# One place modulo 512 bytes for all tiles that the large matmuls read, with tiles shared in MLA, convolution, MLP and compression

## The chip, the cores and the metric

The kernel runs on one core of a Trainium2 chip. The metric is the device time of one execution in microseconds (us), the median of several. Engines: PE (TensorE; its weight loads are PEld), DVE (VectorE), ACT (ScalarE), POOL (GpSimd), SP (SyncE, which here only issues DMAs).

## The reference

Two transformer blocks in float32 over 512 tokens of width 1024. The first block adds 16 meta tokens, the second has two layers.

```
h = concat(meta_tokens, x)
h = h + mixer_block(rms_norm(h))       # differential attention (4 heads) and windowed GQA (8 heads), gated
h = h + swiglu(rms_norm(h))            # 1024 -> 2816 -> 1024
x = rms_norm(h)[:, 16:]
for layer in 0, 1:
    m = mixer_a(rms_norm(x)) if layer == 0 else mixer_c(rms_norm(x))
    x = x + rms_norm(m)
    x = x + rms_norm(relu(rms_norm(x) @ w1)**2 @ w2)   # 1024 -> 4096 -> 1024
# mixer_a: a gated causal convolution of three taps, and MLA (low-rank causal attention, rope)
# mixer_c: NSA: compressed, selected and windowed attention, 16 heads, gated
# short_conv(u)[t] = w[0] u[t-2] + w[1] u[t-1] + w[2] u[t], u = 0 before the start
```

## The kernel before, in words

Activations lie transposed: 128 features on the partitions, 512 tokens along them. Each float32 operand of a large product is split into a high and a low part (`split`: ACT writes the high part, DVE the rest), and `mm3` makes each product of three matmuls for each 128 rows of the contraction: high weights by high data (L189), high by low (L190), low by high (L191). A weight tile of 8 x 128 x 128 is loaded by SP into one of four `wr` tiles (`weights`, L173), split by ACT (L175) and DVE (L176) into `wh` and `wl` (three of each), and used by 24 matmuls of 512 columns. `wh`/`wl` slices are the stationary operand, a slice of 512 bytes a partition; the other tile is the moving operand, 2048 bytes a partition. The moving tiles are: `ah`/`al` (pool `acts`, eight of each; in block 1 with 16 columns more for the meta tokens), `hh`/`hl` (hidden units of feed-forward and MLP), `xh`/`xl` (MLP input, in the right-hand pool `res`), `mh`/`ml`, `yah`, `ybh` (block 1's merge and output), `cqh`, `ckh` (MLA's low ranks). `wxh`/`wxl` are weights loaded ahead, in the right-hand pool.

Pools are stacked from the left in the order in which they are opened: `base`, `raws` (`wr`), `shift` (32 bytes), `splits` (`wh`, `wl`), `shift2` (32 bytes), `acts`, `small` (columns of statistics, 2240 bytes in slots of 32 or 64), then the pools of a stage. `res` is laid from the right end. Each tile takes its bytes a partition, rounded up to 32. `raws` and `splits` are multiples of 512 bytes; a tile of `acts` is 528 x 4 = 2112 bytes, 64 over four times 512; most stage tiles are multiples of 512. In the compiled program of before this gives, as bytes past a multiple of 512:

| Tiles | before | relative to `wh`, `wl` |
|---|---|---|
| `wh`, `wl`, `wxh`, `wxl` | 480 | 0 |
| `xh0` to `xl7` (bytes 174,048 to 206,816 of a partition) | 480 | 0 |
| `ah0`, `al0`, `ah1`, `al1`, ... | 0, 64, 128, 192, ... | 32, 96, 160, 224, ... |
| `hh`, `hl`, `yah`, `yal`, `ybh`, `cqh`, `ckh` | 192 | 224 |
| `mh0` to `ml7` (bytes 157,376 to 190,144) | 192 | 224 |
| `wr` | 448 | 480 |

A pool's tag is a ring of `bufs` slots; a tile that finds no free slot is not written before the last reader of the slot's former tile. Instructions are queued on each engine by the framework's list scheduler, by the order of the code where slots and operands allow it, so a ring that is short changes the order in the queue too.

In block 1 the attention scores go through `sm` (9 slots). The windowed part takes four a step (two groups of heads, four blocks of queries: eight steps; reduction L502), multiplies them on POOL (L515) and hands them to `window_out`, which is run two steps later (`W_LATE`) and transposes them (L524). The differential part takes four a step and runs its output one step later; two of the four are free once added to the others. In MLA the low ranks come first, then the rope tiles `kr` (copied by POOL into `kt`) and `qr`; between the steps of attention the convolution's projections `hv`, `gc`, `gb` run as filling. `rb` of pool `base` (two slots) holds a row of norms spread over the partitions. In NSA, `compress` makes compressed keys and values with a small gelu network (L1258 to L1295).

Of the kernel before, what the change touches and what calls it, by code (L numbers as in the profile page):

```python
# [16 lines left out]
S = 512  # L17
NM = 16
T = S + NM
EPS = 1e-6  # L20
KT = D // 128
# [32 lines left out]
def two_blocks_kernel(ctx: ExitStack, tc: tile.TileContext, w: dict, c: dict, out: bass.AP, dbg=None):  # L54
# [4 lines left out]
    raws = ctx.enter_context(tc.tile_pool(name="raws", bufs=4))  # L59

    shift = ctx.enter_context(tc.tile_pool(name="shift", bufs=1))
    shift.tile([128, 8], F, name="shift0", tag="shift0")
    splits = ctx.enter_context(tc.tile_pool(name="splits", bufs=3))
    shift2 = ctx.enter_context(tc.tile_pool(name="shift2", bufs=1))
    shift2.tile([128, 8], F, name="shift1", tag="shift1")
    acts = ctx.enter_context(tc.tile_pool(name="acts", bufs=1))
    small = ctx.enter_context(tc.tile_pool(name="small", bufs=1))

    def pool(es, name, bufs=1, space=None, side=None):
# [37 lines left out]
    gfp = base.tile([128, KT], F, name="gfp")  # L107
    permr = base.tile([128, 128], R, name="permr")

    def gcol(name, k):  # L110
# [85 lines left out]
    def new_act(k):  # L196
        ah[k] = acts.tile([128, T], R, name=f"ah{k}", tag=f"ah{k}")
        al[k] = acts.tile([128, T], R, name=f"al{k}", tag=f"al{k}")

# [142 lines left out]
    def mul1(dst, src, scalar=1.0):  # L342
        nc.gpsimd.tensor_scalar(dst, src, scalar, 1.0, op0=OP.mult, op1=OP.mult)  # L343
# [15 lines left out]
    def block1(esh):  # L359
# [44 lines left out]

        esi = ExitStack()
        p1 = pool(esi, "b1i")

# [6 lines left out]
        def sm_tile():  # L414
            return p1.tile([128, T], F, name="sm", tag="sm", bufs=9)

        def pt_tile():
            return p1.tile([128, 512], R, name="pt", tag="pt", bufs=8)

# [15 lines left out]
        def values(c0, nh):  # L435

            pv = kv_gemm(c0)
            vf = p1.tile([128, T], F, name="vf", tag="vf", bufs=1)
            for half in range(2):
                nc.scalar.activation(vf[:, 264 * half:264 * half + 264], pv[half], AF.Copy)  # L440
            v = p1.tile([128, 5, nh, 2, 128 // nh], R, name="v2", tag="v2", bufs=2)
            p = t_ps()
            for j in range(4):
                nc.tensor.transpose(p[:, 128 * j:128 * j + 128], vf[:, 128 * j:128 * j + 128], ident)
            pr = p.rearrange("p (j h e) -> p j h e", j=4, h=nh)
            nc.scalar.activation(v[:, 0:4, :, 0, :], pr, AF.Copy)
            nc.vector.tensor_sub(v[:, 0:4, :, 1, :], pr, f32(v[:, 0:4, :, 0, :]))
            pm = t_ps()
            nc.tensor.transpose(pm[:NM, :128], vf[:, S:], ident)
            pr = pm[:NM, :128].rearrange("p (h e) -> p h e", h=nh)  # L450
            nc.scalar.activation(v[:NM, 4, :, 0, :], pr, AF.Copy)
            nc.vector.tensor_sub(v[:NM, 4, :, 1, :], pr, f32(v[:NM, 4, :, 0, :]))
            return v
# [347 lines left out]
    def mlp(hp, hs, xs, norm, wts, layer, pre, ahead):  # L801
# [19 lines left out]
        for grp in range(4):  # L821
            hid = []
            for f in range(8 * grp, 8 * grp + 8):
                if f < 5:
                    q = q0[f]
                else:
                    wt = up(f)
                    q = d_ps()
                    mm3(q, wt, lambda k: xs[k], K8)
                t = p.tile([128, S], F, name="ft", tag="ft", bufs=3)  # L830
                nc.vector.scalar_tensor_tensor(t, q, 0.0, rb, op0=OP.max, op1=OP.mult)
                nc.scalar.activation(t, t, AF.Square)
                a = p.tile([128, S], R, name="hh", tag="hh", bufs=8)
                b = p.tile([128, S], R, name="hl", tag="hl", bufs=8)
                split(a, b, t)
                hid.append((a, b))
# [26 lines left out]
        else:  # L863

            ht = [[acts.tile([128, T], F, name="ht", tag=f"a{x}{j}")[:, :S] for x in "hl"] for j in range(4)]
            mt = [acts.tile([128, T], F, name="mt", tag=f"ah{4 + j}")[:, :S] for j in range(4)]
            rc = tiny(4, "rc")
# [78 lines left out]
    def mla(rc, rb):  # L946
# [17 lines left out]
        def low_rank(name, gname, c0, nk):  # L964
            sq = Squares(p, nk, (("cv", 2), ("avb", 1)))
            res = []
# [14 lines left out]
            nc.vector.tensor_mul(r, r, rc)  # L981
            dst = p.tile([128, S], F, name=f"rb{name}", tag=f"rb{name}")
            return res, row_of(r, a_ps(), dst)
# [16 lines left out]
        def rope_tile(q, r, name):  # L1000
            t = tmp_tile()
            nc.vector.tensor_mul(t, q, r)
            rope(t)
            a = p.tile([128, S], R, name=f"{name}h", tag=f"{name}h")
            b = p.tile([128, S], R, name=f"{name}l", tag=f"{name}l")
            split(a, b, t)
            return a, b
# [17 lines left out]
        def conv(i):  # L1025
            t = []
            for j, nm in enumerate(("hv", "gc", "gb")):
# [4 lines left out]
                if j == 1:  # L1032
                    u = p.tile([128, S + 2], F, name="cu", tag="cu", bufs=1)
                    nc.vector.memset(u[:, 0:2], 0.0)
                    nc.vector.tensor_mul(u[:, 2:], q, rb)
                    nc.gpsimd.tensor_mul(u[:, 2:], u[:, 2:], t[0])
                else:
                    x = p.tile([128, S], F, name="cv", tag="cv", bufs=2)
                    nc.vector.tensor_mul(x, q, rb)
                    t.append(x)  # L1040
# [3 lines left out]
            wc = [gcol("a_conv_w_2", 4 * k + i) for k in range(3)]  # L1044
            mul1(y, u[:, 2:], wc[2])
            nc.vector.scalar_tensor_tensor(y, u[:, 1:S + 1], wc[1], y, op0=OP.mult, op1=OP.add)
            nc.vector.scalar_tensor_tensor(y, u[:, 0:S], wc[0], y, op0=OP.mult, op1=OP.add)
            nc.gpsimd.tensor_mul(y, y, t[1])
# [129 lines left out]
    def nsa(norm, wts, esh):  # L1178
# [20 lines left out]
        nc.scalar.dma_start(qsc, c["c_qs"])  # L1199


        q = first[0][:48]
# [25 lines left out]
        def compress(which):  # L1228
# [25 lines left out]
            for h in range(2):  # L1254
                split(w1p[h][:, :, 0], w1p[h][:, :, 1], raw[:, 8 * h:8 * h + 8])
            w2r = p.tile([64, 64], F, name="w2r", tag="w2r")
            nc.sync.dma_start(w2r, w[f"c_cmp_w2_{name}_2"][0])
            w2h = p.tile([64, 2, 64], R, name="w2h", tag="w2h")  # L1258
            w2l = p.tile([64, 2, 64], R, name="w2l", tag="w2l")
            split(w2h, w2l, w2r[:, None, :].to_broadcast([64, 2, 64]))  # L1260
# [5 lines left out]
            u = p.tile([64, 4, 128], F, name="gelu", tag="sc", bufs=1)  # L1266
            x = p.tile([64, 128], F, name="gx", tag="gx")
            hp = hp.rearrange("p (x n) -> p x n", x=2)
# [8 lines left out]
            nc.vector.scalar_tensor_tensor(u[:, 0], u[:, 3], 1.0, x, op0=OP.add, op1=OP.mult)  # L1277
            hh = p.tile([64, 128], R, name="hdh", tag="hdh")
            hl = p.tile([64, 128], R, name="hdl", tag="hdl")
            split(hh, hl, u[:, 0], scale=0.5)  # L1280
# [274 lines left out]
```

## Time and profile before

| | us |
|---|---|
| median of 3 runs | 2154.07 (2153.51 to 2155.69) |
| profiled execution, its own time | 2153.8 |
| its span, first to last instruction | 2151.7 |
| PE busy | 2091.1 |
| PE weight loads busy | 1706.7 |
| DVE busy | 1151.5 |
| ACT busy | 940.6 |
| POOL busy | 422.1 |

The stages in the span, roughly: norm and first projections to 48 us; windowed attention to 106, differential to 245; gates, merge and output of block 1 to 421; feed-forward to 790; low ranks, MLA and convolution to 1000 and their output to 1056; MLP to 1423; NSA's projections, compression and attention to 1737, output to 1780; MLP to the end.

Busy times count an engine's instructions; matmuls overlap, so the spacing of their starts is shorter than the duration of one. The profile gives the granted TensorE clock for each stretch (1.00 is the upper level, 2.4 GHz).

### The profile page before, as it was taken

How to read it: one execution, taken by the hardware profiler on the slowest of the kernel's cores; microseconds unless marked ns; L12 is line 12 of the kernel's file. 1: busy time of each engine (PE TensorE's matmuls, PEld its weight loads, DVE VectorE, ACT ScalarE, POOL GpSimd, SP SyncE). 2: the span in 40 equal slices, each digit the busy share in tenths (PEclk: the TensorE clock that was granted, in tenths of full speed). 3: DMA queues.
4: the chain of work that ended last, by engine and by line, in shares of the span. 5: the costliest groups of instructions: out<-in, count | busy, mean ns of one | idle time of the engine just before them, and what ended most of it. 6: DMA issues, size and time to landing. Idle time of an engine off the chain costs nothing.

```text
span 2151.7 us, 27008 instructions
## 1 busy us (share of the span) xinstructions
PE 2091.1 (97%) x10214; PEld 1706.7 (79%) x10214; DVE 1151.5 (54%) x1989; ACT 940.6 (44%) x1701; POOL 422.1 (20%) x498
## 2 busy tenths in 40 slices
PE   7999999999999999999999999998999999999998
PEld 6789787888888877777888888886777778888887
DVE  6877633444453454676543343457888847244343
ACT  5755423422222253445443232337767745233232
POOL 2321111200010142332400000154433323000003
PEclk9999999999999999999999999999999999999999
DMA  6122233333333243323323333343111032333331
GB/s 170 45 59 65 89 89 88 88 98 89 98 89 98 84 138 73 79 62 104 92 85 93 97 98 94 96 105 89 30 41 30 11 118 69 98 98 91 96 98 50
DMA packets 351202, 181.96 MB, mean 85 GB/s; under 512 B 42548, under 2 KB 343488, under 8 KB 351072
## 3 DMA queue, kind: packets, MB, share of 16 engines
q1 hardware_dynamic: 344176, 168.55, 27.6%
q10 hardware_dynamic: 6048, 10.63, 1.5%
q8 instruction: 80, 1.31, 0.3%
q0 software_dynamic: 848, 1.06, 0.3%
q14 instruction: 50, 0.41, 0.1%
HBM read 173.92 MB, written 6.29 MB: 84 GB/s over the span
## 4 chain that ended last, share of the span: by engine, by line
PE 86%; DVE 5%; ACT 3%; issue 2%; POOL 2%; DMA 0%; DVEq 0%; SPq 0%; ACTq 0%; POOLq 0%
PE gps L189 14%; PE gps L190 14%; PE gps L191 14%; PE sps L189 6%; PE sps L190 6%; PE sps L191 6%; PE tps L190 5%; PE tps L191 5%; PE tps L189 5%; PE aps L1422 1%; PE tps L1418 1%; ACT pt L208 1%; POOL m L786 1%; PE aps L1423 1%; DVE h L787 1%
## 5 line engine op out<-in xcount | busy, mean ns | idle before, releaser
L175 ACT ACTIVATE wh<-wr 128x1024 fp32r<-128x1024 f32 (+1 forms) x295 | 309.8, 1050 | 828.2 <-PE gps L190 310.6
L176 DVE TENSOR_TENSOR wl<-wr,wh 128x1024 fp32r<-128x1024 f32 (+1 forms) x295 | 388.2, 1316 | 204.7 <-ACT wh L175 201.7
L189 PE MATMUL gps<-ah,wh 128*128 128x512 f32 (+2 forms) x864 | 325.8, 379 | 6.9 <-ACT ah L208 2.4
L190 PE MATMUL gps<-al,wh 128*128 128x512 f32 (+2 forms) x864 | 325.6, 377 | 0.0
L191 PE MATMUL gps<-ah,wl 128*128 128x512 f32 (+2 forms) x864 | 324.5, 376 | 0.8 <-DVE wl L209 0.8
L189 PEld LDWEIGHTS gps<-ah,wh 128*128 128x128 f32 x864 | 163.5, 190 | 35.7 <-ACT ah L208 2.7
L191 PEld LDWEIGHTS gps<-ah,wl 128*128 128x128 f32 x864 | 163.5, 189 | 28.6 <-DVE wl L209 1.2
L190 PEld LDWEIGHTS gps<-al,wh 128*128 128x128 f32 x864 | 163.4, 189 | 25.9 <-issue 0.5
L353 ACT ACTIVATE sm<-sm,nm 128x128 f32<-128x128 f32 (+6 forms) x224 | 130.4, 583 | 38.9 <-DVE nm L1400 19.6
L250 POOL TENSOR_TENSOR sq<-sq 128x512 f32<-128x512 f32 x65 | 96.1, 1483 | 195.3 <-ACT sq L248 193.9
L343 POOL TENSOR_SCALAR m<-m,gc 128x512 f32<-128x512 f32 (+1 forms) x20 | 14.1, 703 | 604.8 <-ACT sq L248 604.8
L343 POOL TENSOR_SCALAR sm<-sm,ri 128x128 f32<-128x128 f32 (+3 forms) x160 | 91.8, 594 | 171.4 <-DVE ri L1407 86.1
L189 PE MATMUL gps<-hh,wh 128*128 128x512 f32 (+1 forms) x306 | 117.5, 384 | 0.0
L190 PE MATMUL gps<-hl,wh 128*128 128x512 f32 (+1 forms) x306 | 117.4, 384 | 0.0
L191 PE MATMUL gps<-hh,wl 128*128 128x512 f32 (+1 forms) x306 | 117.4, 384 | 0.0
L209 DVE TENSOR_TENSOR pt<-tps,pt 128x512 fp32r<-128x512 f32 (+5 forms) x164 | 101.4, 632 | 28.1 <-ACT pt L208 26.6
L208 ACT ACTIVATE pt<-tps 128x512 fp32r<-128x512 f32 (+5 forms) x164 | 87.0, 548 | 63.3 <-PE tps L1418 25.9
L190 PE MATMUL gps<-xl,wh 128*128 128x512 f32 (+1 forms) x240 | 92.5, 385 | 4.9 <-DVE xl L212 4.6
L189 PE MATMUL gps<-xh,wh 128*128 128x512 f32 (+1 forms) x240 | 91.4, 381 | 0.9 <-ACT xh L211 0.9
L191 PE MATMUL gps<-xh,wl 128*128 128x512 f32 (+1 forms) x240 | 91.3, 380 | 0.0
L731 POOL TENSOR_TENSOR ft<-ft 128x512 f32<-128x512 f32 x22 | 29.7, 1352 | 313.6 <-DVE ft L728 297.6
L190 PE MATMUL tps<-hl,wh 128*128 128x512 f32 (+1 forms) x210 | 81.3, 387 | 0.2 <-DVE hl L209 0.2
(512 smaller groups left out, 4677.4 us busy)
## 6 DMA issues: line engine op xcount, KB each, us to landing
wr<-in_mlp_w_dram SPq DMA_DIRECT2D x128, 512.0 KB, 4.0
wr<-in_w_in_dram SPq DMA_DIRECT2D x34, 512.0 KB, 4.0
wr<-in_w_ff_gate_dram SPq DMA_DIRECT2D x22, 512.0 KB, 3.8
wr<-in_w_ff_up_dram SPq DMA_DIRECT2D x22, 512.0 KB, 3.9
wr<-in_a_w_in_dram SPq DMA_DIRECT2D x20, 512.0 KB, 3.9
wr<-in_w_ff_down_dram SPq DMA_DIRECT2D x16, 512.0 KB, 3.9
wr<-in_c_w_in_dram SPq DMA_DIRECT2D x12, 512.0 KB, 4.0
wr<-in_w_out_dram SPq DMA_DIRECT2D x8, 512.0 KB, 3.8
```

What stands on the lines that cost most here:

```text
L175: nc.scalar.activation(wh, raw, AF.Copy)
L176: nc.vector.tensor_sub(wl, raw, f32(wh))
L189: nc.tensor.matmul(ps, wh[:, j, ws], h, start=first and i == 0, stop=False)
L190: nc.tensor.matmul(ps, wh[:, j, ws], l, start=False, stop=False)
L191: nc.tensor.matmul(ps, wl[:, j, ws], h, start=False, stop=last and i == n - 1)
L208: a = nc.scalar.activation(hi, src, AF.Copy)
L209: b = nc.vector.tensor_sub(lo, src, f32(hi))
L250: nc.gpsimd.tensor_add(self.t[0][:, cols], self.t[0][:, cols], t[:, cols])
L343: nc.gpsimd.tensor_scalar(dst, src, scalar, 1.0, op0=OP.mult, op1=OP.mult)
L353: nc.scalar.activation(sm[:, :N], sm[:, :N], AF.Exp, bias=nm, scale=-1.0, accum_out=sums)
L731: nc.gpsimd.tensor_mul(pair[0], pair[0], pair[1])
L786: nc.gpsimd.tensor_mul(m[k][:, c], m[k][:, c], rb[:, c])
```

## The change

The tiles are placed anew. `shift` and `shift2` go; 32 bytes at the end of `base` (`pad0`) keep `splits` where it was and move `raws` by 32. A tile of `acts` becomes 640 x 4 = 2560 bytes, five times 512, of which the first 528 columns are used. `small` gets 320 bytes (`pad1`): 2240 + 320 = 2560. So `acts` and every left pool after `small` start 480 past a multiple of 512. Block 1's `pt` and `v2` go into a pool of their own ahead of the other attention tiles. `cu` loses its two columns in front, so that MLA's tiles stay in step, and `pad2` (192 bytes) does the same for NSA: 32 + 32 + 192 + 768 = 1024.

This takes 7168 + 320 - 32 = 7456 bytes a partition more. Room for it: `sm` in block 1 has 8 slots, not 9; MLP's `ft` lies in the slots of `al4` to `al7`; in MLA `kr` and `qr` share `rh`/`rl`, the row for `cq` goes into an `rb` slot of `base`, the convolution's `hv` lies in its output tile `ys[i]` and `cv` has one slot; in the compression `w2h`, `w2l`, `hh` and `hl` are quarters of one tile in the slot of `pch` or `pcl`, and `gx` is an `sm` tile.

With `cu` two columns shorter, the convolution adds the shifted products only to the columns that have them (511 and 510 of 512), and the zeroing of the two columns goes. What is computed is the same.

```diff
+TP = 640
-    shift = ctx.enter_context(tc.tile_pool(name="shift", bufs=1))
-    shift.tile([128, 8], F, name="shift0", tag="shift0")
     splits = ctx.enter_context(tc.tile_pool(name="splits", bufs=3))
-    shift2 = ctx.enter_context(tc.tile_pool(name="shift2", bufs=1))
-    shift2.tile([128, 8], F, name="shift1", tag="shift1")
     acts = ctx.enter_context(tc.tile_pool(name="acts", bufs=1))
     small = ctx.enter_context(tc.tile_pool(name="small", bufs=1))
+    small.tile([128, 80], F, name="pad1", tag="pad1")
...
+    base.tile([128, 8], F, name="pad0", tag="pad0")
...
     def new_act(k):
-        ah[k] = acts.tile([128, T], R, name=f"ah{k}", tag=f"ah{k}")
-        al[k] = acts.tile([128, T], R, name=f"al{k}", tag=f"al{k}")
+        ah[k] = acts.tile([128, TP], R, name=f"ah{k}", tag=f"ah{k}")[:, :T]
+        al[k] = acts.tile([128, TP], R, name=f"al{k}", tag=f"al{k}")[:, :T]
...
         esi = ExitStack()
+        p0 = pool(esi, "b1p")
         p1 = pool(esi, "b1i")
...
-            return p1.tile([128, T], F, name="sm", tag="sm", bufs=9)
+            return p1.tile([128, T], F, name="sm", tag="sm", bufs=8)
...
-            return p1.tile([128, 512], R, name="pt", tag="pt", bufs=8)
+            return p0.tile([128, 512], R, name="pt", tag="pt", bufs=8)
...
-            v = p1.tile([128, 5, nh, 2, 128 // nh], R, name="v2", tag="v2", bufs=2)
+            v = p0.tile([128, 5, nh, 2, 128 // nh], R, name="v2", tag="v2", bufs=2)
...
-                t = p.tile([128, S], F, name="ft", tag="ft", bufs=3)
+                t = acts.tile([128, TP], F, name="ft", tag=f"al{4 + f % 4}")[:, :S]
...
-            sq = Squares(p, nk, (("cv", 2), ("avb", 1)))
+            sq = Squares(p, nk, (("cv", 1), ("avb", 1)))
...
-            dst = p.tile([128, S], F, name=f"rb{name}", tag=f"rb{name}")
+            dst = p.tile([128, S], F, name=f"rb{name}", tag=f"rb{name}") if name == "ck" else None
...
-            a = p.tile([128, S], R, name=f"{name}h", tag=f"{name}h")
-            b = p.tile([128, S], R, name=f"{name}l", tag=f"{name}l")
+            a = p.tile([128, S], R, name=f"{name}h", tag="rh")
+            b = p.tile([128, S], R, name=f"{name}l", tag="rl")
...
-                    u = p.tile([128, S + 2], F, name="cu", tag="cu", bufs=1)
-                    nc.vector.memset(u[:, 0:2], 0.0)
-                    nc.vector.tensor_mul(u[:, 2:], q, rb)
-                    nc.gpsimd.tensor_mul(u[:, 2:], u[:, 2:], t[0])
+                    u = p.tile([128, S], F, name="cu", tag="cu", bufs=1)
+                    nc.vector.tensor_mul(u, q, rb)
+                    nc.gpsimd.tensor_mul(u, u, t[0])
                 else:
-                    x = p.tile([128, S], F, name="cv", tag="cv", bufs=2)
+                    x = p.tile([128, S], F, name="cv", tag="cv", bufs=1) if j else ys[i]
...
-            mul1(y, u[:, 2:], wc[2])
-            nc.vector.scalar_tensor_tensor(y, u[:, 1:S + 1], wc[1], y, op0=OP.mult, op1=OP.add)
-            nc.vector.scalar_tensor_tensor(y, u[:, 0:S], wc[0], y, op0=OP.mult, op1=OP.add)
+            mul1(y, u, wc[2])
+            for d in (1, 2):
+                nc.vector.scalar_tensor_tensor(y[:, d:], u[:, :S - d], wc[2 - d], y[:, d:], op0=OP.mult, op1=OP.add)
...
+        p.tile([128, 48], F, name="pad2", tag="pad2")
...
-            w2r = p.tile([64, 64], F, name="w2r", tag="w2r")
+            w2r = p.tile([64, 128], F, name="w2r", tag="w2r")[:, :64]
...
-            w2h = p.tile([64, 2, 64], R, name="w2h", tag="w2h")
-            w2l = p.tile([64, 2, 64], R, name="w2l", tag="w2l")
+            part = p.tile([128, S], R, name="w2", tag=("pch", "pcl")[which], bufs=1)[:64].rearrange("p (n c) -> p n c", n=4)
+            w2h, w2l = (part[:, n].rearrange("p (a e) -> p a e", a=2) for n in range(2))
...
-            x = p.tile([64, 128], F, name="gx", tag="gx")
+            x = sm_tile()[:64, :128]
...
-            hh = p.tile([64, 128], R, name="hdh", tag="hdh")
-            hl = p.tile([64, 128], R, name="hdl", tag="hdl")
+            hh, hl = part[:, 2], part[:, 3]
```

## Rows read from the trace of the kernel before

**Rows 1.** The page: span and instructions, and the chain by engine.

```profile
span 2151.7 us, 27008 instructions
...
PE 86%; DVE 5%; ACT 3%; issue 2%; POOL 2%; DMA 0%; DVEq 0%; SPq 0%; ACTq 0%; POOLq 0%
```

**Rows 2.** Windows: stretch, its us, busy (instructions) PE PEld DVE ACT POOL, clock, DMA.

```profile
48.00:106.00 58.00, 57.00 (x307) 42.82 (x306) 48.62 (x131) 44.25 (x116) 16.82 (x28) 1.00 0.18 51
106.00:245.00 139.00, 136.09 (x908) 117.48 (x906) 100.63 (x266) 78.27 (x172) 26.23 (x36) 1.00 0.20 60
...
421.00:790.00 369.00, 368.71 (x1579) 295.76 (x1578) 168.03 (x166) 112.12 (x138) 46.59 (x34) 1.00 0.32 93
...
850.00:1000.00 150.00, 143.28 (x684) 114.24 (x684) 107.72 (x201) 73.44 (x153) 54.83 (x66) 1.00 0.28 73
...
1070.00:1423.00 353.00, 350.49 (x1586) 288.52 (x1585) 149.73 (x173) 120.30 (x164) 31.23 (x29) 0.99 0.32 92
...
1460.00:1737.00 277.00, 259.70 (x1410) 205.10 (x1408) 217.39 (x576) 198.74 (x481) 107.32 (x172) 0.99 0.14 35
```

**Rows 3.** Windows, PE alone: stretches on `xh`, `hh`, `ah` and `mh` only, in this order.

```profile
1147.20:1190.40 43.20, 43.20 (x192) 1.00 0.33 97
1102.60:1145.80 43.20, 43.20 (x187) 1.00 0.31 89
551.60:594.80 43.20, 43.20 (x186) 1.00 0.30 87
...
372.00:408.00 36.00, 36.00 (x156) 1.00 0.28 81
```

**Rows 4.** By tile (`xh`, then `hh`) in those stretches: ns min/median/max, first and last start.

```profile
L189 PE MATMUL tps<-xh,wh x24: 389/389/395, 1147.1 to 1190.0; 128*128 128x512 f32 x24
...
L189 PE MATMUL sps<-hh,wh x24: 395/396/397, 1102.3 to 1146.4; 128*128 128x512 f32 x24
```

**Rows 5.** Groups by form, whole trace: first and last of `ah` (3), `hh` (3), small families (5).

```profile
L191 PE MATMUL gps<-ah,wl 128*128 128x512 f32 x672 | 269.0, 400 | 0.8 <-DVE wl L209 0.8
...
L191 PE MATMUL gps<-hh,wl 128*128 128x512 f32 x274 | 108.4, 395 | 0.0
...
L191 PE MATMUL sps<-hh,wl 128*128 128x512 f32 x188 | 74.3, 395 | 0.0
...
L191 PE MATMUL tps<-ah,wl 128*128 128x512 f32 x128 | 50.7, 396 | 0.5 <-DVE wl L176 0.5
...
L191 PE MATMUL gps<-mh,wl 128*128 128x512 f32 x64 | 25.5, 398 | 0.0
...
L191 PE MATMUL gps<-ckh,wl 128*128 128x512 f32 x16 | 6.3, 396 | 0.0
```

**Rows 6.** Group by form in 48 to 245, and windows of `wl` in MLA and NSA.

```profile
L191 PE MATMUL gps<-ah,wl 128*128 128x512 f32 x71 | 29.0, 408 | 0.0
...
850.00:1000.00 150.00, 59.39 (x150) 1.00 0.28 73
1460.00:1737.00 277.00, 56.12 (x137) 0.99 0.14 35
```

**Rows 7.** Groups by form, whole trace: 264 columns, and 256 on `xl` and `hl`.

```profile
L191 PE MATMUL gps<-ah,wl 128*128 128x264 f32 x160 | 46.6, 292 | 0.0
...
L190 PE MATMUL sps<-xl,wxh 128*128 128x256 f32 x32 | 9.8, 307 | 0.0
...
L190 PE MATMUL gps<-hl,wh 128*128 128x256 f32 x32 | 9.1, 284 | 0.0
```

**Rows 8.** Line L502: the reductions, and idle time of DVE before them (us, times).

```profile
L502 DVE CUSTOM_DVE_ANT_0 sm<-sps,bt,nsink x32: 481/560/635, 47.3 to 105.9; 128x272 f32<-128x272 f32 x16, 128x400 f32<-128x400 f32 x16
...
  PE tps L524: 1.4, 2
```

**Rows 9.** Waits of SP's queue: us in total, times, longest.

```profile
SPq L173 <- DVE wl L176: 1420.6, 264, 25.4
```

**Rows 10.** Line L1048: the convolution's last multiply.

```profile
L1048 POOL TENSOR_TENSOR y<-y,cv x4: 1281/1328/2247, 882.1 to 992.8; 128x512 f32<-128x512 f32 x4
```

More of the change, by code (lines that the diff above doesn't have):

```diff
@@ L863, in mlp @@
         else:
-            ht = [[acts.tile([128, T], F, name="ht", tag=f"a{x}{j}")[:, :S] for x in "hl"] for j in range(4)]
-            mt = [acts.tile([128, T], F, name="mt", tag=f"ah{4 + j}")[:, :S] for j in range(4)]
+            ht = [[acts.tile([128, TP], F, name="ht", tag=f"a{x}{j}")[:, :S] for x in "hl"] for j in range(4)]
+            mt = [acts.tile([128, TP], F, name="mt", tag=f"ah{4 + j}")[:, :S] for j in range(4)]
             rc = tiny(4, "rc")
```

## The prediction

> **What bounds the kernel now.** I read the page's first part and its chain first: the profiled execution spans 2151.7 us, and the chain that ended last runs on PE for 86% [rows 1]. The profiled execution took 2153.8 us, 2.1 us more than its span, and the median of the three runs is 2154.07, 0.3 above it. Then the stretches by stage: in the projections and MLPs PE has no idle time worth naming (368.7 of 369 us, 350.5 of 353), while in the attention stages DVE is busy 72 to 84% of the time and PE is not alone in setting the pace [rows 2]. So in a dense stage the time is the number of matmuls times the spacing of their starts, and the question is whether this spacing depends on the place of the tiles.
>
> It differs by the moving tile. I took stretches that hold matmuls of one family only, 512 columns each, PE busy throughout, granted clock 1.00 in all. Counting instructions that touch the stretch and taking off the 1.7 already under way at its start (a duration of 389 ns over a spacing of 227), the 43.2 us of `xh`/`xl` hold 190.3 starts, a spacing of 227.0 ns; those of `hh`/`hl` 185.3, so 233.1; those of `ah`/`al` 184.3, so 234.4 (one count is worth 1.2 ns, and a neighbouring stretch holds one more, so I take 233.8); 36 us of `mh`/`ml` 154.3, so 233.3 [rows 3]. The duration of one, read by tile, says the same without counting: 389 ns for `xh`, 395 to 397 for `hh` [rows 4].
>
> What do `xh` and `xl` have that the others lack? The table of places above: they alone lie where `wh` and `wl` lie, modulo 512. `hh`, `hl`, `mh`, `ml` and the rest of the left pools lie 224 bytes on, `ah` and `al` at eight places, 32 to 480 bytes on. The weights, the three PSUM pools in turn, shape and clock are the same. It is not that `xh` lies high in SBUF: `mh`/`ml` fill bytes 157,376 to 190,144 of a partition and `xh`/`xl` 174,048 to 206,816, and `mh` has the slow spacing [rows 3].
>
> **The change part by part.** *The place.* After it `wh`, `wl`, `ah`, `al`, and by the padding of `small` all left pools, start at the place that `xh` has now. A matmul of 512 columns on them should then start every 227.0 ns. How many: `ah`/`al` 3 x (672 + 152 + 128) and 24 on `wxh`, 2880; `hh`/`hl` 3 x (274 + 194 + 188) = 1968; the five small families (`mh`, `yah`, `ybh`, `cqh`, `ckh`) 3 x (64 + 32 + 32 + 36 + 16) = 540 [rows 5]. Gain at most 2880 x 6.8 = 19.6, 1968 x 6.1 = 12.0 and 540 x 6.3 = 3.4: 35.0 us. The matmuls on `xh` have the low spacing already.
>
> Of these 5388, 3 x (71 + 150 + 137) = 1074 stand in the attention stages [rows 6], worth 1074 x 6.6 = 7.1 us. The other 27.9 lie where PE is busy end to end, and nothing comes late there instead: the weight DMAs wait for room, not PE for them (SP waits 1420.6 us in total on VectorE's reading of raw tiles) [rows 9]. In attention a spacing counts only where no other engine is awaited; between none and all of the 7.1 I take half, 3.5, since PE is busy 94 to 98% there and DVE 72 to 84% [rows 2].
>
> *Other matmul widths.* 480 matmuls have 264 columns; half of them read from 1056 bytes into the tile, 32 past a multiple of 512, and so won't lie at the common place. Bounded by a 512-column gain scaled by width, 480 x 6.8 x 264/512 = 1.7 us either way; I take 0. For 256 columns the aligned tiles show no advantage: 307 ns on `xl` against 284 on `hl`, the former in a stage that waits for its operands [rows 7]. I take 0. The attention's own matmuls (`pt`, `v2`, `qk`) move too; with no row at equal place to price them, I scale from the large ones: 160 of 512 columns on `pt` in NSA, about 1 us either way, taken as 0.
>
> A rule speaks against all this. The two spacings differ with nothing but the place [rows 3]. The Trainium skill, SBUF — State Buffer, section "SBUF: two separate sides", says that contention on the engine side exists only on the port pair of VectorE and GpSimd, and that TensorE never waits on anyone; its section "A bandwidth-pool intuition that's wrong" gives the weight load a read port of its own. By that, a tile's place could cost nothing, and the sum would be 0. Here rows and rule differ, and I follow the rows; the rule's result is the second rival.
>
> *Sharing in block 1.* Score tiles `sm` go from 9 to 8. The windowed part asks for four a step and keeps two earlier steps, so the ring is already short of 12; a reduction (L502) that finds no slot waits for the transposes that read the tile. Now that is 1.4 us in two waits [rows 8]. The diff costs at most one reduction of 0.56 us on each of the six steps that find the ring full, 3.4 us, and at least nothing, as VectorE has other work; the framework may also queue things in another order, to either side. I take 1.4, the present wait again. The differential part keeps at most one step's two tiles and asks for four: 8 suffice.
>
> *Sharing elsewhere* has one answer each. `ft` on `al4` to `al7`: the last matmuls on these tiles (out_proj's closing) stand ahead of the MLP's on PE's own queue, and `ft` is written only after them; four buffers instead of three. `hv` in `ys[i]` and one `cv`: the next `gb` has to wait for the multiply by the last one (POOL, 1.3 us); these stand (992.8 - 882.1)/3 = 36.9 us apart [rows 10]. `rh`/`rl` for `kr` and `qr`: the copies out of `kr` stand on POOL ahead of the cosine multiply (L997) that `qr` needs anyway; `rqb` takes the `rb` buffer whose reader, the feed-forward's end, is six weight tiles back. `part` in the slot of `pch`/`pcl`, `gx` in `sm`: their next writer depends on the compression's result. The two-column memset goes, and the adds of the convolution are one and two columns shorter: under 0.3 us of DVE beside PE work. Were any of these covers gone, the price would be one wait of 1 to 2 us, at four places at most. Raw weight tiles move by 32 bytes; a slower landing would be hidden by three tiles of 5.4 us loaded ahead.
>
> Sum: 2153.8 - 27.9 - 3.5 + 1.4 = 2123.8 us, and with the 0.3 of the median 2124.1. I say **2124**.
>
> **The rivals.** *The attention stages take back part of it.* They span 58 + 139 + 150 + 277 = 624 us [rows 2], VectorE is their second bound, and other rings and other addresses mean another queue order. If nothing is gained there and 2% is lost, 12.5 us: 2153.8 - 27.9 + 12.5 = 2138.4. For it: DVE at 84% and a ring cut by one. Against: the diff adds no work to any engine, and the ring's present wait is 1.4 us.
>
> *The place is not the cause.* Something else that `xh` has makes 227, such as the absolute place of the right-hand pool, or equal place is needed of more than moving tile and weights. Then 2154 with the sharing's cost, up to 2156. For it: one family alone shows the low spacing, so it rests on one coincidence. The rule of the Trainium skill (SBUF — State Buffer) weighed above would end here too. Against: `mh` is slow at the same height, and the diff reproduces the offset of `xh` exactly, not only equality.
>
> *Slower: the score ring serialises block 1's windowed attention.* Eight tiles hold just two steps. If a step cannot begin until the output of the step before last has been transposed, softmax tail and output stand in line: POOL's four multiplies, then transposes, splits and products. I estimate it at 5 us, two thirds of a step, on each of eight steps that now take 58/8 = 7.3 us [rows 2]. That is 40: 2153.8 - 31.4 + 40 = 2162.4. It decides from (31.4 + 4.3)/8 = 4.5 us a step. For it: the order in the code wants twelve. Against: nine are short too, and the queue already runs the old outputs between the new scores; losing one tile delays one score in four.
>
> **How the numbers follow.** Forecast 0.78, attention takes back 0.13, no effect of the place 0.05, slower 0.04. 0.2%, 4.3 us, is about what a measurement of this kernel can tell from no change. Faster by more than that: 0.78 + 0.13 = 0.91; same 0.05; slower 0.04. The range: below, all of 35.0, 1.7 and 1 from other widths, no cost: 2116. Above, 27.9 alone, 3.4 for the ring and about 8 for a worse order in attention, short of the first rival's full price: 2138.
>
> **What would show it.** Right: `ah`, `hh`, `mh` and `cqh` at 389 ns with 192 starts touching 43.2 us; the feed-forward and MLP stages shorter by 2.7 to 3% for `ah` and `hh` and unchanged for `xh`; counts of weight matmuls unchanged; waits of L502 for L524 up by a few us at most. Wrong: equal place but 395 ns and more (then place is not it), or attention stages longer than 58, 139, 150 and 277 us, with new waits on tiles that share a slot. The prediction fails as a whole if the `ah` and `hh` stretches keep their 233 ns.

## The result and the profile after

The changed kernel takes 2127.56 us, median of four executions (2124.1 to 2128.88), the kernel before 2153.85 beside it: a ratio of 0.9874, 95% interval 0.9857 to 0.9891. The forecast was 2124, range 2116 to 2138. The profiled execution took 2126.7 us with a span of 2124.9, 26.8 less than before.

The page of the changed kernel, answering to [rows 1]: span, and the chain by engine.

```profile
span 2124.9 us, 26991 instructions
...
PE 86%; DVE 5%; ACT 3%; issue 3%; POOL 2%; DMA 0%; SPq 0%; ACTq 0%; DVEq 0%; POOLq 0%
```

PE carries the chain as before; it only gets through sooner. Windows of PE alone, on `xh`, `hh`, `ah` and `mh` in the order of [rows 3] (stretch, its us, busy and instructions that touch it, clock, DMA):

```profile
1125.70:1168.90 43.20, 43.20 (x193) 1.00 0.33 97
1082.10:1125.30 43.20, 43.20 (x192) 1.00 0.36 104
560.00:603.20 43.20, 43.20 (x192) 1.00 0.33 96
370.00:406.00 36.00, 36.00 (x161) 1.00 0.30 88
```

`hh` went from 187 to 192, `ah` from 186 to 192, `mh` from 156 to 161; `xh` holds 193 against 192, one count, at the same clock. The duration of one, by tile, is that of `xh` for all (answers to [rows 4]; ns min/median/max):

```profile
L188 PE MATMUL tps<-xh,wh x24: 389/389/389, 1125.6 to 1168.4; 128*128 128x512 f32 x24
...
L188 PE MATMUL sps<-hh,wh x24: 389/389/389, 1082.1 to 1124.9; 128*128 128x512 f32 x24
...
L188 PE MATMUL gps<-ah,wh x30: 389/389/389, 560.2 to 601.7; 128*128 128x512 f32 x30
...
L190 PE MATMUL gps<-mh,wl x54: 389/389/389, 369.9 to 405.9; 128*128 128x512 f32 x54
```

A sharper reading than counts is the first and last start of an unbroken run of one family. 192 matmuls on `hh` span 44.56 us before and 43.29 after, so 233.3 and 226.7 ns over 191 gaps; 384 on `ah` 89.58 and 86.81 (233.9 and 226.7); 192 on `xh` 43.32 and 43.29. Below, a spacing is worked out this way.

The stretches of [rows 2], each moved and shortened with its stage:

```profile
48.00:106.00 58.00, 57.25 (x314) 43.61 (x313) 47.84 (x126) 43.49 (x114) 17.53 (x30) 1.00 0.18 51
106.00:245.00 139.00, 135.55 (x905) 116.98 (x903) 103.33 (x271) 78.65 (x174) 25.74 (x35) 1.00 0.20 60
416.00:774.00 358.00, 357.61 (x1579) 295.57 (x1578) 168.83 (x165) 111.77 (x137) 46.47 (x34) 1.00 0.33 96
831.60:980.40 148.80, 141.46 (x684) 114.21 (x684) 108.02 (x198) 73.38 (x153) 55.44 (x66) 1.00 0.28 73
1050.00:1398.00 348.00, 345.29 (x1587) 288.29 (x1586) 149.54 (x173) 119.65 (x164) 31.03 (x29) 1.00 0.33 93
1433.50:1714.50 281.00, 261.66 (x1417) 207.68 (x1415) 218.85 (x579) 199.88 (x483) 108.92 (x172) 0.99 0.14 35
```

The same 1579 matmuls of the feed-forward's stretch now take 358 us instead of 369, the 1586 or 1587 around the first MLP 348 instead of 353. Block 1's attention is as long as it was, and NSA's stretch takes 281 us instead of 277. By the starts of the matmuls that mark each stage, in us (the difference taken before rounding; share: the sharing alone, own: the version with places modulo 256, second profile, both below):

| Stage | before | after | after − before | share | own |
|---|---|---|---|---|---|
| to the first windowed score | 46.8 | 46.7 | −0.1 | 46.6 | 45.5 |
| windowed and differential, to the last `pt` | 191.1 | 190.8 | −0.3 | 190.9 | 190.9 |
| gates, to the first `mh` | 127.1 | 123.7 | −3.4 | 127.2 | 123.7 |
| merge, output, to the first `hh` | 141.6 | 137.8 | −3.8 | 141.6 | 137.8 |
| feed-forward, first to last `hh` | 281.0 | 272.7 | −8.2 | 280.9 | 272.8 |
| to the first `cqh` | 60.8 | 58.3 | −2.5 | 59.3 | 58.3 |
| low ranks, MLA, to the last `pt` | 161.0 | 159.8 | −1.2 | 161.6 | 159.9 |
| output, to the first `xh` | 39.9 | 39.3 | −0.6 | 39.9 | 39.4 |
| first MLP, to the last `hh` | 364.4 | 359.7 | −4.7 | 364.5 | 359.7 |
| NSA, to the last `pt` | 320.4 | 322.9 | **+2.4** | 324.0 | 319.4 |
| output, to the first `xh` | 38.6 | 39.0 | +0.4 | 38.7 | 40.2 |
| second MLP, to the end | 378.8 | 374.2 | −4.6 | 378.8 | 374.1 |

All stages with large products gain but NSA's output, which differs by 1.1 between two profiles of the changed kernel, and NSA itself, which loses. Where NSA loses, three readings say. The matmuls on PE between the end of the first MLP and NSA's first score, in the changed kernel, then in the last version, which has the compression's own tiles (stretch, us, busy and instructions, clock, DMA):

```profile
1388.80:1472.90 84.10, 70.37 (x348) 0.92 0.42 98
```

```profile
1388.00:1472.80 84.80, 76.09 (x363) 0.90 0.42 99
```

Sharing puts 15 matmuls fewer ahead of the first score; the queues stand in another order. The second reading is VectorE's timeline in the changed kernel, from the second compression's gelu to its hidden tile (start, us, line):

```profile
1474.83 0.28 DVE L1273 TENSOR_TENSOR sm<-gelu 64x128 f32<-64x128 f32 x1
1475.03 0.74 DVE L1308 SCALAR_TENSOR_TENSOR gps<-gps,qsc,rb 128x512 f32<-128x512 f32 x1
1475.69 0.27 DVE L1274 TENSOR_SCALAR sm<-sm 64x128 f32<-64x128 f32 x1
1475.89 1.21 DVE L208 TENSOR_TENSOR wl<-wr,wh 128x1024 fp32r<-128x1024 f32 x1
...
1477.41 0.69 DVE L1313 TENSOR_TENSOR qk<-gps,qk 64x512 fp32r<-64x512 f32 x1
1478.13 0.37 DVE L1277 TENSOR_TENSOR gelu<-gelu,sm 64x128 f32<-64x128 f32 x1
1478.76 0.69 DVE L1313 TENSOR_TENSOR qk<-gps,qk 64x512 fp32r<-64x512 f32 x1 [0.26 <-ACT qk L1312]
1479.48 0.29 DVE L1279 SCALAR_TENSOR_TENSOR gelu<-gelu,sm 64x128 f32<-64x128 f32 x1
1480.15 0.69 DVE L208 TENSOR_TENSOR pt<-tps,pt 128x512 fp32r<-128x512 f32 x1 [0.38 <-ACT pt L207]
1480.76 0.27 DVE L211 SCALAR_TENSOR_TENSOR w<-gelu,w 64x128 fp32r<-64x128 f32 x1
```

Between the steps of this short chain stand five large instructions of the projections and the attention (0.74 + 1.21 + 0.69 + 0.69 + 0.69 = 4.0 us). Its last step starts 91.9 us after the first MLP's last matmul on `hh` (1480.76 − 1388.8). With the compression's own tiles the chain meets other neighbours:

```profile
1472.52 0.28 DVE L1273 TENSOR_TENSOR gx<-gelu 64x128 f32<-64x128 f32 x1
1472.92 0.69 DVE L1314 TENSOR_TENSOR qk<-gps,qk 64x512 fp32r<-64x512 f32 x1
...
1475.26 0.28 DVE L1277 TENSOR_TENSOR gelu<-gelu,gx 64x128 f32<-64x128 f32 x1
...
1476.10 0.28 DVE L1279 SCALAR_TENSOR_TENSOR gelu<-gelu,gx 64x128 f32<-64x128 f32 x1 [0.35 <-ACT gelu L1278]
...
1476.78 0.28 DVE L211 SCALAR_TENSOR_TENSOR hdl<-gelu,hdh 64x128 fp32r<-64x128 f32 x1
```

That is 88.8 us after the first MLP (1476.78 − 1388.0). On PE the product of this tile stands directly ahead of the first compressed score (`kc` by `qk`), and the third reading is that score to the last `pt`, in the changed kernel and in the last version:

```profile
1481.50:1711.70 230.20, 221.83 (x1243) 1.00 0.10 26
```

```profile
1477.00:1707.30 230.30, 222.14 (x1245) 1.00 0.10 26
```

It takes the same time in both, so NSA lost its time ahead of this score. From the first to the last of the steps shown the chain takes 5.9 us instead of 4.3, as in the kernel before, and the product follows the last step's start by 0.5 us instead of beginning with it: 2.2 us, and so to 0.1 us in all eight profiles of kernels that share as the diff does. The rest lies in when the chain starts: 84.1 to 87.3 us after the first MLP in these eight, 86.0 and 87.3 in two profiles of the changed kernel, 84.5 and 84.6 in two of the last version. What moves it no run shows.

### The profile page after: what moved, and what is told of

Read it like the earlier page. It is cut to its first block, busy times and chain, and to the rows that moved or that the text cites. A ratio compares the mean times of both kernels' runs of the same rounds, so it can differ in the third digit from the quotient of the medians.

```text
span 2124.9 us, 26991 instructions
## 1 busy us (share of the span) xinstructions
PE 2060.9 (97%) x10214; PEld 1708.7 (80%) x10214; DVE 1156.2 (54%) x1985; ACT 937.8 (44%) x1701; POOL 423.3 (20%) x498
## 4 chain that ended last, share of the span: by engine, by line
PE 86%; DVE 5%; ACT 3%; issue 3%; POOL 2%; DMA 0%; SPq 0%; ACTq 0%; DVEq 0%; POOLq 0%
PE gps L188 14%; PE gps L190 14%; PE gps L189 14%; PE sps L188 6%; PE sps L189 6%; PE sps L190 6%; PE tps L189 5%; PE tps L188 5%; PE tps L190 5%; PE tps L1419 1%; PE aps L1423 1%; DVE h L787 1%; ACT sm L352 1%; POOL qk L342 1%; PE aps L1424 1%
## 5 line engine op out<-in xcount | busy, mean ns | idle before, releaser
L190 PE MATMUL gps<-ah,wl 128*128 128x512 f32 (+2 forms) x864 | 321.9, 373 | 2.2 <-DVE wl L208 2.2
L208 DVE TENSOR_TENSOR pt<-tps,pt 128x512 fp32r<-128x512 f32 (+5 forms) x164 | 101.5, 633 | 27.9 <-ACT pt L207 26.5
L189 PE MATMUL gps<-xl,wh 128*128 128x512 f32 (+1 forms) x240 | 92.7, 386 | 5.3 <-DVE xl L211 4.9
```

The lines of the kernel that those rows point to most:

```text
L189: nc.tensor.matmul(ps, wh[:, j, ws], l, start=False, stop=False)
L190: nc.tensor.matmul(ps, wl[:, j, ws], h, start=False, stop=last and i == n - 1)
L208: b = nc.vector.tensor_sub(lo, src, f32(hi))
```

## The experiments

**The sharing alone.** The places of before, with every other edit of the diff. Against the changed kernel:

```diff
-TP = 640
...
+    shift = ctx.enter_context(tc.tile_pool(name="shift", bufs=1))
+    shift.tile([128, 8], F, name="shift0", tag="shift0")
     splits = ctx.enter_context(tc.tile_pool(name="splits", bufs=3))
+    shift2 = ctx.enter_context(tc.tile_pool(name="shift2", bufs=1))
+    shift2.tile([128, 8], F, name="shift1", tag="shift1")
...
-    small.tile([128, 80], F, name="pad1", tag="pad1")
...
-        ah[k] = acts.tile([128, TP], R, name=f"ah{k}", tag=f"ah{k}")[:, :T]
+        ah[k] = acts.tile([128, T], R, name=f"ah{k}", tag=f"ah{k}")
...
```

> The sharing of the diff alone (sm 8, ft on al4 to al7, one cv, hv in its output tile, rb for cq, rh/rl shared, shorter cu, the compression's quarters and gx), with no padding: ah/al are 2112 bytes again, weights and stage tiles lie 32 to 480 bytes apart as in the kernel before. My theory (the place gives the spacing, the sharing gives nothing): spacing of ah, hh and mh 233 to 234 ns as before, 2154 us, or up to 2158 if the 4.0 us that NSA's compression lost in the changed kernel come from the sharing. Rival (the sharing and its new queue order bring the gain): 2127 us.

2157.43 us (2154.92 to 2162.12, ten executions), ratio 1.0014, interval 1.0004 to 1.0025. Windows on `hh` and `ah`:

```profile
1101.00:1144.20 43.20, 43.20 (x187) 1.00 0.35 98
551.10:594.30 43.20, 43.20 (x187) 1.00 0.30 87
```

The runs of `hh` and `ah` span 44.56 and 89.58 us, as before to the hundredth. So the spacing is none of the sharing's doing. In all the sharing costs 0.1%, with 3.6 us lost in NSA and 1.6 gained ahead of the first `cqh` (column share). Block 1's two stages lost nothing with eight score tiles.

**The hidden tiles displaced.** A pad in front of `hh`/`hl`, all else as in the changed kernel. In the first kernel it takes 224 bytes in the feed-forward, 32 and 256 in the two MLPs:

```diff
         p = pool(es, "ff")
+        p.tile([128, 56], F, name="pad3", tag="pad3")
...
         p = pool(es, "mlp")
+        p.tile([128, (8, 64)[layer]], F, name="pad4", tag="pad4")
```

> The changed kernel, with only the hidden tiles hh/hl moved by a pad in their pool: in the feed-forward 224 bytes from the common place (where before had them), in the first MLP 32, in the second MLP 256. ah, xh and weights stay. My theory (distance between moving tile and weights modulo 512): the feed-forward's 528 hidden matmuls go from 227 back to 233 ns, +3.2 us; the MLPs' 768 each by 1 to 8 ns at 32 (ah0 had 230 there) and at 256 some 1 to 8 as well, so +1 to +6 each: 2132 to 2142 us in all, with ah and xh at 227 beside them. Rival (what counts is that the pools as a whole are aligned, or something of the new queue order): 227 ns for hh everywhere, 2127.

> As the run before, with other distances: feed-forward 64 bytes, first MLP 128, second MLP 480. By distance modulo 512: each stage of its own spacing between 228 and 237 ns for hh, 2129 to 2144 us in all. Rival (distance counts only modulo 64): 227 at 64 and 128, and slow, 233 or so, only at 480. Rival (only that the tile is displaced at all): the same 233 in all three.

Windows of 43.2 us on the hidden tiles: feed-forward, first MLP, second MLP. At 224, 32 and 256 bytes:

```profile
498.90:542.10 43.20, 43.20 (x187) 1.00 0.30 88
1085.50:1128.70 43.20, 43.20 (x187) 1.00 0.35 97
1812.60:1855.80 43.20, 43.20 (x192) 1.00 0.38 105
```

In the second kernel, at 64, 128 and 480 bytes:

```profile
499.60:542.80 43.20, 43.20 (x191) 1.00 0.32 94
1086.00:1129.20 43.20, 43.20 (x187) 1.00 0.34 97
1810.30:1853.50 43.20, 43.20 (x187) 1.00 0.34 97
```

From the spans of 192 matmuls: 226.7 ns at 0 and at 256, 229.0 at 64, 233.3 at 32, 128, 224 and 480. Runs of `xh` keep 226.7 to 226.9 in both. The totals, 2135.48 and 2137.88, lie within what the distances say. Displacing one family slows that family alone, and the pools being aligned as a whole is not what counts. What was not foreseen is 256: as good as 0. By duration, again, 395 ns at 224 and 389 at 256:

```profile
L188 PE MATMUL gps<-hh,wh x30: 395/396/397, 498.8 to 541.5; 128*128 128x512 f32 x30
...
L188 PE MATMUL gps<-hh,wh x24: 389/389/389, 1823.4 to 1849.9; 128*128 128x512 f32 x24
```

**Everything at another place.** Weights, `ah`/`al`, left pools, `xh` and `wxh` together at 448 instead of 480 (`pad0` taken out, a pad of 32 bytes in the right-hand pool).

> The changed kernel with everything, weights, ah/al, left pools, xh and wx tiles, moved together from 480 to 448 past a multiple of 512. My theory (equality of moving tile and weights is what counts): 227 ns for every family, 2127 us. Rival (the absolute place 480 is what counts, as xh had it before): about 233 ns for every family, xh too, 2127 + 6556 x 6 ns = 2166 us at most, less in attention.

Windows on `hh`, `xh` and `ah`:

```profile
1081.20:1124.40 43.20, 43.20 (x192) 1.00 0.37 104
1124.80:1168.00 43.20, 43.20 (x193) 1.00 0.33 98
542.10:585.30 43.20, 43.20 (x192) 1.00 0.33 96
```

All at 226.7 ns, 2123.07 us: between these two absolute places there is no difference. That it is some 4 us faster than the changed kernel's median I don't claim: its stages are those of the changed kernel to 0.1 us but four that also differ between two profiles of the changed kernel (to the first score, to the first `cqh`, NSA and its output).

**Steps of 64.** `ah`/`al` at 2112 bytes again (`TP` back to `T`), the rest at the common place.

> The changed kernel with ah/al back at 2112 bytes, so that they lie at 64, 128, ... 448 bytes from the weights (ah at 0, 128, 256, 384, al at 64, 192, 320, 448), each in a quarter of the products of its kind; all else at the common place. Known so far, distance and spacing: 0 and 256 give 227 ns, 64 gives 229, 32, 128, 224 and 480 give 234. Theory A (the distance counts modulo 256): 0 and 256 at 227, 64 and 320 alike (229), 128 and 384 alike (234), 192 and 448 alike; ah+al lose 8 to 10 us, 2135 to 2137. Theory B (modulo 512, 256 being good by another reason): the pairs differ. Theory C (the displaced tile in the hidden runs cost by something else than distance): 227 throughout, 2127.

2134.93 us. A window on `ah`/`al`:

```profile
545.50:588.70 43.20, 43.20 (x189) 1.00 0.31 90
```

The run of 384 on `ah`/`al` spans 88.53 us, 231.2 ns. Sorted by the distance of the moving tile and that of the next one, the median gaps of this run in ns are:

| distance → next | ns | 256 further | ns |
|---|---|---|---|
| 0 → 64 | 229 | 256 → 320 | 228 |
| 0 → 128 | 233 | 256 → 384 | 234 |
| 64 → 0 | 228 | 320 → 256 | 228 |
| 128 → 256 | 232 | 384 → 0 | 231 |
| 128 → 192 | 231 | 384 → 448 | 232 |
| 192 → 128 | 234 | 448 → 384 | 233 |

Pairs 256 apart agree within 1 ns, as theory A has it: the distance counts modulo 256. A single gap is weak evidence, though. At one constant distance the gaps go up and down by turns, 231 or 232 and 235 ns at 224 bytes (feed-forward of the first kernel above), 229 or 230 and 237 or 238 at 128 (first MLP of the second), so only means over a run belong to a distance. And in the kernel before, at odd multiples of 32, one pair does not agree: 228 ns after `ah0` (32 → 96), 235 after `ah2` (288 → 352). For constant distances the rule rests on two pairs of means: 0 and 256 (226.7), 224 and 480 (233.3).

**What NSA lost.** Two kernels, each with one edit in the compression:

```diff
-            part = p.tile([128, S], R, name="w2", tag=("pch", "pcl")[which], bufs=1)[:64].rearrange("p (n c) -> p n c", n=4)
+            part = p.tile([128, S], R, name="w2", tag="pch", bufs=1)[:64].rearrange("p (n c) -> p n c", n=4)
...
-            x = sm_tile()[:64, :128]
+            x = p.tile([64, 128], F, name="gx", tag="w2r")
```

> The changed kernel, but w2h, w2l and the hidden tiles of both compressions (of keys, of values) lie in the slot of pch, so that the second waits for the first as it did when they had one slot each. Theory (the 4.0 us that NSA lost come from the second compression's splits having been queued ahead of the first's end, since its quarters lie in the other slot): first score to last pt back from 238.8 to about 235 us, 2123 us. Rival (gx as an sm tile, or the slots of pch and pcl being taken at all): 239 us, 2127.

> The changed kernel, but gx lies in the slot of w2r, not in the ring of sm. Theory (the quarters' slots are the cause): NSA's first score to last pt stays at 239 us, 2127 us. Rival (gx takes a score tile's slot and holds the scores up): 235 us, 2123.

2125.56 us (2124.39 to 2126.11) with the first edit, 2129.0 (one execution) with the second. From the end of the first MLP to the last `pt` NSA takes 321.9 and 324.6 us. The kernels that share as the diff does took 320.9 to 324.2 there (seven profiles: the changed kernel twice, the kernels displaced, at 448, in steps of 64 and with the sharing modulo 256 below). Both lie in that spread or at its edge, so the two runs don't tell which of the two edits is to blame. Split at the first compressed score both differ from the rest: it comes 94.2 and 88.4 us after the first MLP (92.7 in the changed kernel, 89.0 in the last version), and from there to the last `pt` they take 227.7 and 236.2 us, every other kernel 230.1 to 230.6. What either edit gives in one part it changes the other way in the other. The order on PE is the quarters' doing: with the first edit 364 matmuls touch the stretch ahead of the first score, much as in the last version (363), with the second 348 as in the changed kernel. Here my expectations measured wrongly, too: they count from the first score, which itself comes after 348 instead of 363 matmuls, so part of "4.0 us" was work moved across the mark.

**Modulo 256, and the compression's tiles its own.** 576 columns for an `ah`/`al` tile and 64 bytes of padding in `small` are enough for distances of 0 and 256. The 4352 bytes that this saves give `w2h`, `w2l`, the hidden tiles and `gx` their own places back:

```diff
-TP = 640
+TP = 576
...
-    small.tile([128, 80], F, name="pad1", tag="pad1")
+    small.tile([128, 16], F, name="pad1", tag="pad1")
...
-            x = sm_tile()[:64, :128]
+            x = p.tile([64, 128], F, name="gx", tag="gx")
...
```

> A tile of ah/al takes 2304 bytes (576 columns), small 2304, so that all moving tiles lie at 0 or 256 bytes from the weights modulo 512: ah, xh at 0, al and all left stage pools at 256. The room won (4352 bytes) gives the compression its own w2h, w2l, hidden tiles and gx back; the other sharing stays. Theory (distance counts modulo 256, and the sharing in the compression costs 4.0 us): 227 ns for all families, NSA's first score to last pt 235 us, 2123 us. Rival (only 0 modulo 512 is good, the hidden run's 227 at 256 being special to it): al and the stage tiles above 230, 2140 us. Rival (the NSA loss is not from the compression's sharing): 227 ns, but 239 us, 2127.

> The changed kernel once more, beside the next run on the same chip: 2127 us, a ratio to before near 0.987. Both theories of the next run are measured against it.

> The kernel with places modulo 256 and the compression's own tiles once more. Theory (it wins back what NSA lost, 4 us): 2122 to 2123 us, a ratio to before near 0.985, its interval below that of the changed kernel. Rival (the difference of some 5 us between two sessions was the chip's): the same ratio as the changed kernel, 0.987.

> The kernel with places modulo 256, but with the compression's sharing as in the changed kernel. Theory (the sharing alone costs NSA's 4 us, whatever the places): first score to last pt 239 us, 2126 to 2127 us. Rival (the 4 us came from the full pool and its places): 234 to 235 us, 2122.

First 2122.02 us, ratio 0.9847. Then beside the changed kernel on one chip: 2123.54 (2121.61 to 2123.84), ratio 0.9852, against 2128.05 (2124.5 to 2129.33), ratio 0.9873. The intervals of the ratios (0.9836 to 0.9869, 0.9858 to 0.9888) overlap, though no execution of the one reaches any of the other, in eight each over the sessions. It beats both kernels. Windows on `hh`, `xh` and `ah`, whose tiles now lie 256, 0 and (`al`) 256 from the weights:

```profile
1081.20:1124.40 43.20, 43.20 (x192) 1.00 0.37 105
1124.80:1168.00 43.20, 43.20 (x192) 1.00 0.33 97
541.50:584.70 43.20, 43.20 (x192) 1.00 0.33 96
```

NSA takes 319.2 and 319.4 us in the two profiles, shorter than in any kernel that shares in the compression: the sharing costs 1.6 to 4.9 us, 3.0 on average over the seven profiles, of which 2.2 are the longer chain and the later product. With the sharing, modulo 256 too, the one execution took 2124.59 and NSA 321.0, 1.7 more with this edit alone: the places are not at fault, but its total is below what I expected, as this stretch came out at the low end.

**The weights alone.** In that version `wh` and `wl` moved by 32 bytes. The two pads make 256 together, so `ah`/`al` and the left pools behind them move by 256, at which the spacing is the same; `xh` and `wxh` stay:

```diff
+    shift = ctx.enter_context(tc.tile_pool(name="shift", bufs=1))
+    shift.tile([128, 8], F, name="shift0", tag="shift0")
     splits = ctx.enter_context(tc.tile_pool(name="splits", bufs=3))
+    shift2 = ctx.enter_context(tc.tile_pool(name="shift2", bufs=1))
+    shift2.tile([128, 56], F, name="shift1", tag="shift1")
```

> The kernel of the run before with wh and wl alone moved by 32 bytes; every moving tile keeps its place, and wxh/wxl keep theirs. Theory (the distance between moving tile and weights counts, no place of either by itself): all moving tiles are now 224 or 480 bytes from wh/wl, so about 234 ns for all of them, xh too, and 227 only in the products on wxh/wxl; some 6500 x 6.5 ns = 42 us, less what attention hides, 2157 to 2164 us. Rival (it is enough that the moving tiles share a place among themselves): 227 ns, 2122 us.

2164.3 us, 40.8 more. Windows on `hh`, `xh` and `ah`:

```profile
1102.10:1145.30 43.20, 43.20 (x187) 1.00 0.34 94
1146.90:1190.10 43.20, 43.20 (x187) 1.00 0.31 88
550.40:593.60 43.20, 43.20 (x187) 1.00 0.30 87
```

Every family is slow, `xh` among them, which no kernel had slow before: it is the distance from moving tile to weights. The program has 6756 matmuls of 512 columns on `wh`/`wl`; by 6.7 ns they are 45.3 us, so nine tenths of it reach the end (one execution).

## Why the prediction was right, and where its terms were off

**What bounds.** Right: a dense stage takes the number of matmuls by their spacing, and nothing came late in its place. SP still waits for VectorE's reading of raw tiles, 1420.6 us before [rows 9], now:

```profile
SPq L172 <- DVE wl L175: 1391.3, 265, 25.4
```

**The dense term.** 27.9 was forecast; the stages outside the three attentions gained 27.7 (the sum of their rows before rounding); the projections that open NSA's stretch are not in it. Of this, 1.6 ahead of the first `cqh` came with the sharing alone too, in a stretch that differs by 0.6 between two profiles of the changed kernel. The counts were right. The gains per matmul were a little larger than the 6.8 and 6.1 read from [rows 3]: 7.2 for `ah` and 6.7 for `hh`, by first and last starts, which beat counts of instructions that touch a window.

**The attention term** was somewhat too large. Half of 7.1 us was taken, 3.5. In the last version, where the compression has its own tiles, block 1 gained 0.3, MLA 1.1 and NSA's whole stretch, projections included, 1.1: 2.5. MLA still shares there, and the sharing alone made it 0.6 longer, so of the place alone some 3 us would be left, an estimate. Block 1 gained least: 0.3 of 3 x 71 x 6.6 = 1.4 us, though PE is busy 98% of the time there [rows 2]. So a busy PE does not set the pace alone in that stage.

**The ring of eight.** 1.4 us was taken; the sharing alone left block 1 at 190.9 against 191.1. In the changed kernel VectorE's wait for the transposes ahead of L502 is 0.7 us, where it was 1.4 [rows 8] (idle time of DVE before it, us, times):

```profile
  PE tps L524: 0.7, 2
```

The slower rival, 40 us from this ring, did not appear at all.

**Sharing elsewhere.** This is the step that failed. "`part` in the slot of `pch`/`pcl`, `gx` in `sm`: their next writer depends on the compression's result" weighed the slots' readers and writers only, and gave 0. It cost 3.0 us on average. One of the prediction's signs of being wrong, an attention stage longer than before, came true for this one stage: 281 us against 277. 2.2 of the 3.0 us stand in the longer chain and its later product, and go with the queue order that the first rival names: other slots, another order on VectorE and PE, and a chain of short steps with 4.0 us of other work between them. The rest is the chain's varying start, its cause open. That rival's price was 12.5 us; a quarter came, at one place. The rest of the sharing shows no cost beyond 0.6 us in MLA.

**The sum.** With this term, the attention's, the ring's and the dense term's, 2123.8 becomes 2123.8 + 3.0 + (3.5 − 2.5) − 1.4 + (27.9 − 27.7) = 2126.6, beside the 2126.7 of the profiled execution. That the forecast came within 0.2% of the median is in part luck: the 1.4 us that the ring did not cost stood against the 4.0 that sharing and attention did.

**Widths of 264 and 256.** Zero was right as a sum. By duration, in the changed kernel:

```profile
L190 PE MATMUL gps<-ah,wl 128*128 128x264 f32 x160 | 46.2, 290 | 0.0
...
L189 PE MATMUL gps<-hl,wh 128*128 128x256 f32 x32 | 9.1, 285 | 0.0
```

290 ns against 292 and 285 against 284 [rows 7]. By the median gap between two such matmuls in a row, those of 264 columns went from 122 to 120 ns and those of 256 columns on `hh`/`hl` from 117 to 120: at this width equal place is not better. Over 480 matmuls of the one kind and 480 of the other (on `ah`/`al` and `hh`/`hl`) that is about 1 us each way, an estimate.

**The place is not the cause** is out, in both of its forms: the absolute place (all at 448, same spacing; weights alone moved, `xh` slow where it lay) and something needed beyond moving tile and weights (hidden tiles displaced, that family alone slow). By the rule of the Trainium skill weighed ahead (SBUF — State Buffer, "SBUF: two separate sides") weights moved by 32 bytes would cost nothing; here they cost 40.8 us, and the measurement decides. What in the chip makes the distance count no run shows. The reason as I gave it, equality modulo 512, was sufficient but too narrow: 256 does as well.

## What to carry to other kernels

When two groups of the same instruction have different spacing at the same clock, list what differs, the addresses too: 3% of a PE-bound stage lay in where two operands stand to each other, and one run with the weights alone displaced prices it. Look for the weakest condition that gives the gain (here 256 instead of 512), since room costs something elsewhere. Where a scheduler orders the queues, shared slots can cost time even if their readers and writers never meet: look for the short chain that other work can slip into, and measure a stage between marks that the change does not move.

## What the runs showed of the hardware

At granted clock 1.00 the mean spacing of 128x512 float32 matmuls with a weight load each depends on the distance of moving tile and weights in SBUF: 226.7 ns at 0 and 256 bytes, 229.0 at 64, 233.3 at 32, 128, 224 and 480. That it repeats every 256 bytes is shown for 0 and 256, for 224 and 480 and, in mixed runs, for steps of 64. At equal place it is 226.7 for all families, whatever the pool and the height in SBUF. No family's mean went below that; the Trainium skill (TensorE: Matmul & The Clock Gate, "Back-to-back issue gap") gives about 216 ns for an isolated gap of 512 columns and about 131 for a stream with weight loads, neither of which a run here reached.
